# Two heads to a score pass in the forgetting attention, gate and up weights of an expert in one matmul and neighbouring rows in one packet, and the modulation's sums in three bf16 parts

## The chip, the cores and the metric

The kernel runs on one core of one Trainium2 chip. The metric is the device time of one execution in microseconds (us). The core has a matrix engine (PE, with its weight loads shown apart as PEld), a vector engine (DVE), a scalar engine (ACT), GpSimd (POOL), and queues that issue transfers (SP mostly, POOL for gathers and scatters). Transfers are carried out by 16 DMA engines, and the profile counts their packets.

## What is computed

512 tokens of width 1024 go through two layers of a first block and one layer of a second block, all in fp32. The parts that the change touches are these:

```python
mod = (silu(c) @ w_ada[i] + b_ada[i]).reshape(b, 6, d)      # modulation, two layers

def forgetting_mixer(h, ...):                               # layer 1: 16 heads of 64, causal
    logits = q @ k.T + (c_i[..., None] - cum[:, :, None, :])
    p = softmax(where(mask, logits, -1e30));  o = p @ v

def hierarchical_moe(h, ...):                               # both layers: 16 experts, width 256
    g_idx = argmax(softmax(t @ wg_r + bg_r)); top-2 of the 4 experts of that group
    hid = silu(t @ w_gate[e]) * (t @ w_up[e])               # 1024 -> 256, twice
    y += gate * (hid @ w_down[e])                           # 256 -> 1024
```

## The kernel before

The program runs in stages, and their times in the profiled execution are: layer 0's dilated attention (about 60 to 665 us), its output projection and router (to 722), its experts (to about 920), layer 1's forgetting attention (925 to 1245), output projection and router (to 1297), experts (to 1500), and the second block (to 1847).

**Products in three terms.** Almost every fp32 product is made of three matmuls on split operands (`split3`, L150, the matmul itself is L153): high x high, high x low, low x high. The split is an ACT copy into a reduced fp32 form (L315) and a DVE subtraction (L316).

**PE's order** is written by hand: in the attention stages a planner, `weave`, runs generators in lanes on a virtual clock. Each generator yields a cost and a delay from the table `DL` (in thousands), and while no lane is ready the planner emits background work, the next projections. The other engines' orders come from a scheduler.

**Modulation.** `ada_steps` (L232) reads 8 blocks of 128x512 of `w_ada`, and DVE accumulates them into `adacc` (L246, L248). Then four matmuls with a column of ones (L261) add up the 128 partitions, and DVE adds the bias (L264). 20 of the 24 blocks run as a lane in the dilated attention.

**Forgetting attention.** `mix_b` handles the heads in 8 pairs. A pair's projection, rows of q and k, and scores are lanes. `attn_forget` (L1367) handles one head: for each of 4 blocks of 128 queries it multiplies over the head's 64 dimensions (64 partitions) against 128 to 512 keys, three matmuls, then adds the causal mask with a bf16 matmul of an identity with a mask (`identb`, `maskb`, L1385, 128 partitions). DVE adds the bias and takes the sums (`pexp`, L473), ACT the exponential (L474); then `attn_values` transposes and multiplies with v. Score tiles `sc` are one of 3 buffers in PSUM. In the dilated attention both heads of a pair already take turns, one on the upper and one on the lower 64 partitions (L548).

**Experts.** `expert_loads` (L976) issues six transfers of 512 KB for each expert on SP's queue: gate and up in two halves each (k blocks of 128 rows, so that a packet is one row of 256 numbers, 1 KB), down in two (rows of 1024 numbers, 4 KB). `expert_split` makes high and low parts, except for expert 0. For an expert, `token_list` builds the list of at most 96 tokens from a one-hot matrix (L949), `token_gates` its gates (L957), POOL gathers the rows (L961). `step` runs `expert_half` (L1014) for gate and for up, each 8 k blocks x 3 matmuls of 256 columns; between the halves stand the next expert's transposes. Then come SiLU (L1026), the product, and the down projection (`expert_out`), whose rows POOL scatters and adds into `xd` (L966). Gathers read from `hd`, to which the router wrote the normed rows `hn` (L1194).

**The overflow branch.** `overflow` reads a flag on every engine and branches (L1070, L1071); its body is not entered here. It stands behind expert 0's transposes (L1008) and copies (`xTf`, L1010).

## Time and profile before

| | |
|---|---|
| Time, median of 3 runs | 1851.56 us (1849.99 to 1854.08) |
| Profiled execution | 1848.67 us, its span 1846.8 us |
| Mean granted clock of PE | 0.954 |
| PE busy | 1665.7 us (90%) |
| DVE busy | 1282.6 us (69%) |
| ACT busy | 926.5 us (50%) |
| POOL busy | 121.0 us (7%) |

The profile's span is 1.9 us shorter than the execution's own time. Busy shares are averages over the stages, and a stage has its own limit.

### The profile page before, as it was taken

The page shows a single profiled execution, that of the slowest core. Times are in us where ns is not written, and L with a number is a line of the kernel's source. Part 1 is how long each engine was busy: PE and PEld are TensorE (multiplying, and loading weights), DVE is VectorE, ACT ScalarE, POOL GpSimd, SP SyncE. Part 2 cuts the span into 40 slices and gives each one's busy share as a digit, 9 for nine tenths or more (in the row PEclk, how much of TensorE's full clock was granted, in tenths as well). Part 3 has the DMA queues.
Part 4 walks back from the last instruction along what each step waited for, and adds up shares of the span by engine and source line. Part 5 has one row for each costly group of instructions (what it writes and reads, how often), then busy time and mean ns, then how long its engine had stood idle before and what let it go on. Part 6 is the DMA issues. An engine that isn't in the chain of part 4 may idle for free. (4 is left out here: it accounts for less than half of the span.)

```text
span 1846.8 us, 30370 instructions
## 1 busy us (share of the span) xinstructions
PE 1665.7 (90%) x11022; PEld 1469.2 (80%) x11023; DVE 1282.6 (69%) x3181; ACT 926.5 (50%) x1978; POOL 121.0 (7%) x95
## 2 busy tenths in 40 slices
PE   5979999999999996999869999999598959999998
PEld 3878998989989985787658798888487748788886
DVE  6748777767686657787656667666687755998574
ACT  4536556555565643566444555552465533454443
POOL 1000000000000001133200000000133210000000
PEclk9989999999999997999988899899799979999999
DMA  8886655556564136899753221126699953333331
GB/s 291 244 276 183 189 159 176 164 154 195 153 184 132 58 113 211 270 316 302 208 148 93 58 69 58 63 70 212 197 315 313 295 154 110 98 105 88 112 118 76
DMA packets 294141, 310.83 MB, mean 168 GB/s; under 512 B 31263, under 2 KB 240779, under 8 KB 293980
## 3 DMA queue, kind: packets, MB, share of 16 engines
q1 hardware_dynamic: 286428, 291.88, 51.0%
q0 software_dynamic: 7552, 16.89, 4.2%
q8 instruction: 90, 1.47, 0.3%
q14 instruction: 71, 0.58, 0.1%
HBM read 287.62 MB, written 38.90 MB: 177 GB/s over the span
## 5 line engine op out<-in xcount | busy, mean ns | idle before, releaser
L153 PE MATMUL mm<-whi,hThi 128*128 128x384 f32 (+2 forms) x1128 | 403.3, 358 | 5.4 <-ACT hThi L739 2.0
L153 PE MATMUL mm<-whi,hTlo 128*128 128x384 f32 (+2 forms) x1128 | 384.3, 341 | 1.0 <-DVE hTlo L740 0.5
L153 PE MATMUL mm<-wlo,hThi 128*128 128x384 f32 (+2 forms) x1128 | 382.6, 339 | 0.0
L316 DVE TENSOR_TENSOR wlo<-wst,whi 128x768 fp32r<-128x768 f32 (+2 forms) x200 | 200.1, 1011 | 67.5 <-ACT whi L315 65.0
L153 PEld LDWEIGHTS mm<-whi,hThi 128*128 128x128 f32 x1128 | 215.6, 191 | 13.9 <-ACT hThi L739 3.2
L315 ACT ACTIVATE whi<-wst 128x768 fp32r<-128x768 f32 (+2 forms) x200 | 176.6, 892 | 87.6 <-PE mm L153 54.2
L153 PEld LDWEIGHTS mm<-whi,hTlo 128*128 128x128 f32 x1128 | 214.9, 191 | 6.2 <-DVE hTlo L740 3.3
L316 DVE TENSOR_TENSOR ehl<-est,ehl 128x1024 fp32r<-128x1024 f32 x144 | 175.8, 1222 | 60.8 <-ACT ehl L315 60.1
L153 PEld LDWEIGHTS mm<-wlo,hThi 128*128 128x128 f32 x1128 | 216.0, 191 | 1.9 <-issue 0.6
L315 ACT ACTIVATE ehl<-est 128x1024 fp32r<-128x1024 f32 x144 | 152.1, 1058 | 105.0 <-PE sc L153 23.3
L153 PE MATMUL mm<-ehl,xTh 128*96 128x256 f32 x960 | 178.4, 287 | 0.0
L248 DVE SCALAR_TENSOR_TENSOR adacc<-ast,csil,adacc 128x512 f32<-128x512 f32 x168 | 126.1, 751 | 64.9 <-DMA ast<-in_w_ada_dram 62.9
L153 PE MATMUL mm<-ehl,xTl 128*96 128x256 f32 x480 | 136.0, 283 | 0.0
L153 PEld LDWEIGHTS mm<-ehl,xTh 128*96 128x96 f32 x960 | 134.7, 165 | 0.0
L153 PE MATMUL mm<-hThi,whi 128*128 128x512 f32 (+1 forms) x288 | 107.2, 372 | 0.7 <-ACT sza L1887 0.6
L153 PE MATMUL mm<-hTlo,whi 128*128 128x512 f32 (+1 forms) x288 | 106.0, 368 | 0.5 <-DVE hTlo L310 0.3
L153 PE MATMUL mm<-hThi,wlo 128*128 128x512 f32 (+1 forms) x288 | 105.8, 367 | 0.0
L415 ACT ACTIVATE raw<-mm 128x256 f32<-128x256 f32 x126 | 48.2, 382 | 110.2 <-PE mm L153 109.8
L420 DVE TENSOR_REDUCE qss<-sq 128x4 f32<-128x256 f32 x128 | 53.0, 414 | 63.3 <-ACT sq L417 63.1
L153 PEld LDWEIGHTS mm<-ehl,xTl 128*96 128x96 f32 x480 | 79.0, 165 | 0.0
L1226 POOL MEMSET xg<- 96x1024 f32 x6 | 5.5, 952 | 1066.5 <-PE sc L153 1066.5
L966 POOL DMA_INDIRECT xd<-y,tidx x32 | 66.6, 2083 | 112.8 <-DVE hTl L1048 87.4
(488 smaller groups left out, 3568.0 us busy)
## 6 DMA issues: line engine op xcount, KB each, us to landing
ast<-in_w_ada_dram SPq DMA_DIRECT2D x192, 256.0 KB
wst<-in_a_w_in_dram SPq DMA_DIRECT2D x192, 192.0 KB
est<-in_w_gate_dram SPq DMA_DIRECT2D x64, 512.0 KB
est<-in_w_up_dram SPq DMA_DIRECT2D x60, 512.0 KB
wst<-in_w_in_dram SPq DMA_DIRECT2D x32, 512.0 KB
est<-in_w_down_dram SPq DMA_DIRECT2D x30, 512.0 KB
esp<-in_w_down_dram SPq DMA_DIRECT2D x30, 512.0 KB
wst<-in_b_w_in_dram SPq DMA_DIRECT2D x64, 192.0 KB
```

Source lines behind the costliest of these rows:

```text
L153: self.nc.tensor.matmul(out, lhsT=l, rhs=r, start=n_first and i == 0, stop=n_last and i == nt - 1)
L248: last = nc.vector.scalar_tensor_tensor(acc, st, self.csil[:, k:k + 1], acc, op0=ALU.mult, op1=ALU.add)
L315: nc.scalar.activation(hi, st, AF.Copy)
L316: nc.vector.tensor_sub(lo, st, hi.bitcast(F32))
L415: nc.scalar.activation(raw[:, t].rearrange("p a b -> p (a b)"), p[:, :256], AF.Copy)
L420: nc.vector.tensor_reduce(ss[:, 4 * t:4 * t + 4], sq.rearrange("p (g d) -> p g d", d=HD), axis=AX.X, op=ALU.add)
L966: self.nc.gpsimd.indirect_dma_start(out=dst, out_offset=bass.IndirectOffsetOnAxis(ap=idx, axis=0), in_=src, in_offset=None, bounds_check=S ...
L1226: nc.gpsimd.memset(xg, 0.0)
```

## The change

Seven edits go together.

1. **Scores of two heads.** `forget_scores` replaces the first half of `attn_forget`: both heads of a pair alternate matmul by matmul on the two halves of the partitions, in the groups of query blocks (0,1), (2), (3). The mask is added by 64-partition matmuls (`idh`, `maskh`), which POOL's queue loads by four transfers in `mix_b`. `forget_values` is a lane of its own; `DL` has new delays `bs` and `bp`; `pexp` has two buffers.
2. **Gate and up joined.** `expert_part` does gate and up in one matmul of 512 columns; it runs for k blocks 0 to 3, then the next expert's transposes, then 4 to 7.
3. **Neighbouring rows.** Partition p holds rows 8p to 8p+7. A tile holds two rows of gate and two of up, by two transfers of 256 KB whose packets are 2 KB. To match, L1194's result goes permuted into a second tile.
4. **Token list and gates in one product** for experts 2 to 15.
5. **Overflow's branch earlier,** ahead of the first expert's transposes and loads.
6. **The modulation's sums.** For the 20 blocks in the dilated attention POOL makes three bf16 parts of `adacc` (three copies, two subtractions, each on the result of the one before), and 12 bf16 matmuls add them up. `adacc` has one buffer.
7. **Small tiles** of `merge` have one buffer in place of two. The diff leaves out these, moved indices, and what it removes of `attn_forget` and `expert_loads`, which stand above.

```diff
@@ -42,6 +42,7 @@
+DL.update({'bs': 1.5, 'bp': 3.0})
@@ -248,9 +249,16 @@
                 self.ada_ins.append(last)
+        terms = [(acc, self.ones[:, 0:1])]
+        if later is True:
+            parts = self.t(pool, [P, 3, 512], BF16, "adp", 1)
+            for i in range(3):
+                nc.gpsimd.tensor_copy(parts[:, i], acc)
+                if i < 2:
+                    nc.gpsimd.tensor_sub(acc, acc, parts[:, i])
+            terms = [(parts[:, i], self.onesb[:, 0:1]) for i in range(3)]
         if later:
             yield 0, DL["ad"]
-        terms = [(acc, self.ones[:, 0:1])]
         if n_pe:
@@ -856,8 +864,9 @@
-                              ("tg", [P, NT, 16, 3], BF16)):
+                              ("tg", [P, NT, 16, 5], BF16)):
...
+        self.nc.gpsimd.tensor_copy(R["tg"][:, :, :, 0:2], self.tokv.unsqueeze(2).to_broadcast([P, NT, 16, 2]))
@@ -946,8 +955,11 @@
         for t in range(NT):
-            nc.tensor.matmul(p[:q, 0:2], lhsT=oh[:, t], rhs=self.tokv[:, t], start=t == 0, stop=t == NT - 1)
+            r = self.tokv[:, t] if tg is None else tg[:, t]
+            nc.tensor.matmul(p[:q, 0:r.shape[-1]], lhsT=oh[:, t], rhs=r, start=t == 0, stop=t == NT - 1)
         nc.vector.tensor_scalar(idx, p[:q, 0:1], p[:q, 1:2], 4096.0, op0=ALU.add, op1=ALU.add)
+        if tg is not None:
+            nc.vector.tensor_reduce(gate, p[:q, 2:5], axis=AX.X, op=ALU.add)
         return oh
@@ -976,28 +988,34 @@
+            for c in range(6):
+                plain = c == 5
+                shp = [P, 2, 2, F] if c < 4 else [P, 1, D]
+                j = i - DL["n0"]
+                if 0 <= j < DL["nx"]:
+                    st = self.t(self.px, shp, F32, f"x{j}")
+                else:
+                    st = self.t(self.ws, shp, F32, "esp" if plain else "est", DL["npl"] if plain else DL["nes"])
+                i += 1
+                if c < 4:
+                    for q, nm in enumerate(("w_gate", "w_up")):
+                        nc.sync.dma_start(st[:, q].rearrange("p k f -> p (k f)"),
+                                          dram_ap(a[nm], (l * 16 + e) * D * F + c * 2 * F, [[KC * F, P], [1, 2 * F]]))
+                else:
+                    nc.sync.dma_start(st, dram_ap(a["w_down"], (l * 16 + e) * D * F + (c - 4) * P * D, [[D, P], [P * D, 1], [1, D]]))
+                self.staged.append((self.W[e], st))
+                yield
...
+            pick = (lambda x: [x[:, :, k] for k in range(2)]) if len(w) < 4 else (lambda x: [x[:, 0]])
...
+                w.append([(x,) for x in pick(st)])
...
+            w.append(list(zip(pick(hl[:, 0]), pick(hl[:, 1]))))
@@ -1011,14 +1029,16 @@
-    def expert_half(self, p, o, x, w):
-        for k in range(KC):
+    def expert_part(self, p, x, w, ks):
+        w = [y for c in w[:4] for y in c]
+        for k in ks:
...
-            self.split3(p[:self.CAP, o:o + 256], terms, k == 0, k == KC - 1)
+            self.split3(p[:self.CAP].rearrange("p (a b) -> p a b", a=2), terms, k == 0, k == KC - 1)
@@ -1191,8 +1211,10 @@
                 self.route_tile(pn, lg[:, t], R, t)
-                nc.vector.scalar_tensor_tensor(h, h, r, shrow, op0=ALU.mult, op1=ALU.add)
-                nc.sync.dma_start(hd[ts, :], h)
+                ho = self.t(pn, [P, D], F32, "hn", 3)
+                by = lambda x: x.rearrange("p (q k) -> p k q", k=KC)
+                nc.vector.scalar_tensor_tensor(ho.rearrange("p (k q) -> p k q", k=KC), by(h), r, by(shrow), op0=ALU.mult, op1=ALU.add)
+                nc.sync.dma_start(hd[ts, :], ho)
                 if t == 0:
@@ -1228,15 +1250,15 @@
-            def listed(e):
+            def listed(e, both=False):
...
-                    ohs = self.token_list(pm, R["rk"][:, :, e], idx[:, e:e + 1], self.CAP)
+                    g = dict(tg=R["tg"][:, :, e], gate=gates[:, e:e + 1]) if both else {}
+                    ohs = self.token_list(pm, R["rk"][:, :, e], idx[:, e:e + 1], self.CAP, **g)
...
-                if e < 16:
-                    self.token_gates(ohs, [R["tg"][:, t, e] for t in range(NT)], gates[:, e:e + 1], self.CAP)
+                self.token_gates(ohs, [R["tg"][:, t, e, 2:5] for t in range(NT)], gates[:, e:e + 1], self.CAP)
@@ -1244,12 +1266,11 @@
                     p = self.mm()
-                    self.expert_half(p, 0, xs[e], w[0] + w[1])
+                    self.expert_part(p, xs[e], w, range(4))
                     if e < 15:
                         xs[e + 1] = self.expert_in(pm, xgs[(e + 1) % 3])
-                    self.expert_half(p, 256, xs.pop(e), w[2] + w[3])
-                    ohs = listed(e + 3)
-                    gated(e + 3, ohs)
+                    self.expert_part(p, xs.pop(e), w, range(4, KC))
+                    listed(e + 3, True)
                     hid = self.expert_hidden(pm, p)
@@ -1260,17 +1281,16 @@
+            ohs.append(listed(1))
...
-            load(2)
-            ohs.append(listed(1))
-            load(2)
+            self.overflow(pm, R, hd, l)
+            load(4)
...
-            self.overflow(pm, R, hd, l)
...
-            ohs.append(listed(2))
+            listed(2, True)
...
-            for e in range(3):
+            for e in range(2):
@@ -1364,37 +1384,57 @@
+    def forget_scores(self, pool, u, hp, before, then):
+        nc = self.nc
+        while not (u.get("rows") and self.have_cum and (before is None or before["done"])):
...
+        bias = [self.t(pool, [P, S], F32, f"biasF{h}", 1) for h in range(2)]
+        for h in range(2):
+            nc.sync.dma_start(bias[h], dram_ap(self.ncum, (2 * hp + h) * S, [[0, P], [1, S]]))
...
+        hs = [slice(h * HD, (h + 1) * HD) for h in range(2)]
+        z = [self.t(pool, [P, NT], F32, f"fzz{h}", 2) for h in range(2)]
+        d = [self.t(pool, [P, NT], F32, f"fdd{h}", 2) for h in range(2)]
+        blocks = [[], []]
+        for bs in ((0, 1), (2,), (3,)):
+            p = [self.sc(), self.sc()]
+            o, cost = 0, 300
+            for b in bs:
+                n = (b + 1) * P
+                q = slice(b * P, n)
+                for i, (x, y) in enumerate(((qh, kh), (qh, kl), (ql, kh))):
+                    for h in range(2):
+                        nc.tensor.matmul(p[h][:, o:o + n], lhsT=x[hs[h], q], rhs=y[hs[h], :n], start=i == 0, stop=False)
+                for c in range(2):
+                    for h in range(2):
+                        nc.tensor.matmul(p[h][:, o + b * P:o + n], lhsT=self.idh[hs[h], c], rhs=self.maskh[hs[h], c],
+                                         start=False, stop=c == 1)
+                o += n
+                cost += 200 + 1.4 * n
+            for h in range(2):
+                o = 0
+                for b in bs:
+                    n = (b + 1) * P
+                    e = self.t(pool, [P, n], F32, f"pexp{h}{b}", 2)
+                    self.softmax_piece(p[h][:, o:o + n], bias[h][:, :n], e, z[h][:, b:b + 1], d[h][:, b:b + 1], n)
+                    nc.vector.reciprocal(d[h][:, b:b + 1], d[h][:, b:b + 1])
+                    nc.vector.tensor_scalar(e, e, d[h][:, b:b + 1], None, op0=ALU.mult)
+                    blocks[h] += [e[:, k * P:(k + 1) * P] for k in range(b + 1)]
+                    o += n
+            if bs[-1] == NT - 1:
+                u["scored"] = 2
+            yield cost, DL["bs"]
+        then(blocks)
+    def forget_values(self, pool, u, hp, oT, blocks):
+        nc = self.nc
...
+        hs = [slice(h * HD, (h + 1) * HD) for h in range(2)]
+        terms = [[(vh, vl, kb, b * (b + 1) // 2 + kb) for kb in range(b + 1)] for b in range(NT)]
+        yield from self.attn_values(pool, "b", blocks, hs, terms, lambda h, o: nc.scalar.activation(oT[hs[h], hp], o, AF.Copy))
+        u["done"] = 2
@@ -1413,6 +1453,11 @@
+            self.idh, self.maskh = [self.t(pq, [P, 2, P], BF16, nm) for nm in ("idh", "maskh")]
+            for out, off in ((self.idh, OFF_ID), (self.maskh, OFF_MASK)):
+                for h in range(2):
+                    nc.gpsimd.dma_start(out[h * HD:(h + 1) * HD],
+                                        dram_ap(self.a["c_tab"], off, [[N_CONST, HD], [HD * N_CONST, 2], [1, P]]))
@@ -1449,8 +1494,8 @@
-                    for h in range(2):
-                        fg.append((h, self.attn_forget(pa, u, hp, h, oT), DL["bu"] + h * DL["bo"]))
+                    fg.append(("scores", self.forget_scores(pa, u, hp, hist[hp - 2] if hp > 1 else None, lambda blocks: fg.append(
+                        ("values", self.forget_values(pa, u, hp, oT, blocks), DL["bp"]))), DL["bu"]))
@@ -2158,7 +2199,7 @@
-                self.dilated(po, pa, hT, oT, first, begun, [lambda l=l, cb=cb: self.ada_steps(pa, l, cb, later=True) for l, cb in todo])
+                self.dilated(po, pa, hT, oT, first, begun, [lambda l=l, cb=cb: self.ada_steps(pa, l, cb, n_st=2, n_acc=1, later=True) for l, cb in todo])
...
```

The order of three places follows, before and then after the change.

PE in the forgetting attention, the first head's first two query blocks before (`sc` is the score tile, `kTh`/`kTl` the keys' high and low parts):

```order
L153 MATMUL sc_12291<-kTh_2537_12260,qTh_2534_12245 128x128
L153 MATMUL sc_12291<-kTl_2538_12261,qTh_2534_12245 128x128
L153 MATMUL sc_12291<-kTh_2537_12260,qTl_2535_12246 128x128
L1385 LDWEIGHTS identb_432
L1385 MATMUL sc_12291<-maskb_434,identb_432 128x128
L153 MATMUL sc_12301<-kTh_2537_12260,qTh_2534_12245 128x256
L153 MATMUL sc_12301<-kTl_2538_12261,qTh_2534_12245 128x256
L153 MATMUL sc_12301<-kTh_2537_12260,qTl_2535_12246 128x256
L1385 LDWEIGHTS identb_432
L1385 MATMUL sc_12301<-maskb_434,identb_432 128x128
```

PE at the same place after (two score tiles, one for each head):

```order
L1409 MATMUL sc_12208<-kTh_2547_12173,qTh_2544_12158 128x128
L1409 MATMUL sc_12209<-kTh_2547_12173,qTh_2544_12158 128x128
L1409 MATMUL sc_12208<-kTl_2548_12174,qTh_2544_12158 128x128
L1409 MATMUL sc_12209<-kTl_2548_12174,qTh_2544_12158 128x128
L1409 MATMUL sc_12208<-kTh_2547_12173,qTl_2545_12159 128x128
L1409 MATMUL sc_12209<-kTh_2547_12173,qTl_2545_12159 128x128
L1412 LDWEIGHTS idh_11518
L1412 MATMUL sc_12208<-maskh_11519,idh_11518 128x128
L1412 LDWEIGHTS idh_11518
L1412 MATMUL sc_12209<-maskh_11519,idh_11518 128x128
L1412 LDWEIGHTS idh_11518
L1412 MATMUL sc_12208<-maskh_11519,idh_11518 128x128
```

The two heads alternate, and the mask of a block is four matmuls in place of one. The groups that follow, (2) and (3), stand behind 12 projection matmuls each at this place.

PE in the dilated attention, where the modulation's sum stands before, in the middle of a projection:

```order
L153 MATMUL mm_5116<-whi_4684,hTlo_325 128x384
L261 MATMUL tp_5133<-ones_65,adacc_5009 128x1 x4
L153 MATMUL mm_5116<-whi_4684,hThi_324 128x384
```

PE at such a place after (the start of the 12 bf16 matmuls), and then POOL ahead of it:

```order
L154 MATMUL av_1536<-pTl_1483,vhi_219_862 64x128
L154 MATMUL av_1536<-pTh_1482,vlo_220_863 64x128
L269 LDWEIGHTS adp_1430
L269 MATMUL tp_1562<-onesb_430,adp_1430 128x1
L269 LDWEIGHTS adp_1430
L269 MATMUL tp_1562<-onesb_430,adp_1430 128x1
L269 LDWEIGHTS adp_1430
L269 MATMUL tp_1562<-onesb_430,adp_1430 128x1
```

```order
L256 CAST adp_1430<-adacc_1407 128x512
L258 TENSOR_TENSOR adacc_1407<-adacc_1407,adp_1430 128x512
L256 CAST adp_1430<-adacc_1407 128x512
L258 TENSOR_TENSOR adacc_1407<-adacc_1407,adp_1430 128x512
L256 CAST adp_1430<-adacc_1407 128x512
```

The sum is 12 weight loads and matmuls where there were 4, and they read what POOL's fifth instruction leaves.

ACT at the start of layer 0's experts before, from the last early splits of weights to the branch (`x` and `est` are weight tiles, `tp` the transposes of expert 0's rows):

```order
L315 ACTIVATE ehl_9560<-x_1781_8750 128x1024
L315 ACTIVATE ehl_9565<-x_1809_8885 128x1024
L1010 ACTIVATE xTf_8985<-tp_8986 128x384
L1010 ACTIVATE xTf_8985<-tp_8992 128x384
L1070 TENSOR_LOAD rt_anyi_8937
L1071 COMPARE_AND_BRANCH
```

ACT there after, with the branch's body left out:

```order
L323 ACTIVATE ehl_9838<-x_1802_9037 128x1024
L323 ACTIVATE ehl_9844<-x_1831_9174 128x1024
L323 ACTIVATE ehl_9851<-est_9712 128x1024
L1090 TENSOR_LOAD rt_anyi_9226
L1091 COMPARE_AND_BRANCH
...
L1028 ACT_TABLE_LOAD
L1028 ACTIVATE xTf_9726<-tp_9727 128x384
L323 ACTIVATE ehl_9857<-est_9715 128x1024
L1028 ACTIVATE xTf_9726<-tp_9733 128x384
L323 ACTIVATE ehl_9863<-est_9718 128x1024
```

The copies of expert 0's rows moved behind the branch and behind one more split, of a tile that SP issues just ahead of its own branch, and a table load now stands ahead of them.

## Rows read from the trace of the kernel before

**Rows 1.** Windows: the two attentions, then both experts' stages; columns in us, then clock, DMA share, GB/s.

```profile
140.00:660.00 520.00, 503.12 (x3762) 479.37 (x3760) 370.74 (x950) 295.86 (x756) 0.00 (x0) 1.00 0.52 155
945.00:1245.00 300.00, 290.89 (x1901) 252.38 (x1900) 194.26 (x632) 153.25 (x383) 0.00 (x0) 0.94 0.24 68
770.00:920.00 150.00, 139.78 (x1003) 114.55 (x1001) 114.98 (x171) 85.07 (x132) 44.14 (x25) 0.99 0.93 281
1340.00:1480.00 140.00, 130.36 (x959) 109.18 (x959) 113.02 (x164) 84.77 (x127) 42.65 (x24) 0.98 0.99 304
```

**Rows 2.** Chain that ended last: start us, us, what; layer 1's experts, second block.

```profile
1352.08 2.83 PE mm L153 x24
1355.05 0.18 PE tp L957 x4
...
1370.78 13.54 DMA est<-in_w_down_dram
...
1817.26 10.88 PE mm L153 x48
```

**Rows 3.** SiLU of the 16 experts, layer 0, then layer 1.

```profile
L1026 ACT ACTIVATE sg<-mm x16: 361/380/383, 751.0 to 915.0; 96x256 f32<-96x256 f32 x16
...
L1026 ACT ACTIVATE sg<-mm x16: 364/381/383, 1325.5 to 1488.7; 96x256 f32<-96x256 f32 x16
```

**Rows 4.** Main DMA queue in 1560:1580, 1340:1380 and 1260:1300: packets, MB, share.

```profile
q1 hardware_dynamic: 3312, 2.23, 39.2%
...
q1 hardware_dynamic: 8052, 10.49, 80.2%
...
q1 hardware_dynamic: 3712, 7.87, 56.0%
```

**Rows 5.** PE's longest wait at the start of layer 0's experts.

```profile
PE tp L949 <- PEq L1071: 5.6, 1, 5.6
```

**Rows 6.** Timeline of ACT, then of PE, at the start of layer 0's experts.

```profile
733.99 1.06 ACT L315 ACTIVATE ehl<-est 128x1024 fp32r<-128x1024 f32 x1 [1.09 <-DMA est<-in_w_gate_dram]
749.75 1.28 ACT L1026 ACT_TABLE_LOAD   x1
...
736.97 1.15 PE L153 MATMUL mm<-est,xTf 128*96 128x256 f32 x2
```

**Rows 7.** L1194 by source: count, min/median/max ns, first and last start.

```profile
L1194 DVE SCALAR_TENSOR_TENSOR hn<-hn,tn_r,rh x8: 1274/1277/1283, 691.8 to 1291.7; 128x1024 f32<-128x1024 f32 x8
```

**Rows 8.** Timeline in the dilated attention: bf16 sums of `merge`, last `adacc`, its sum.

```profile
164.14 0.56 PE L640 MATMUL tp<-s,perm 128*128 128x12 bf16 x16
...
199.75 0.75 DVE L248 SCALAR_TENSOR_TENSOR adacc<-ast,csil,adacc 128x512 f32<-128x512 f32 x1
...
205.66 0.95 PE L261 MATMUL tp<-ones,adacc 128*128 128x1 f32 x8
```

**Rows 9.** POOL by line, an instruction of 128x512.

```profile
L1638 POOL MEMSET tt<- 128x512 f32 x1 | 0.5, 528 | 0.0
```

**Rows 10.** Timeline of PE: one head's scores, then a dilated pair's.

```profile
1046.62 0.32 PE L153 MATMUL sc<-kTh,qTh 64*128 64x128 f32 x1
...
1049.77 0.64 PE L153 MATMUL mm<-whi,hThi 128*128 128x384 f32 x1
...
605.92 0.39 PE L548 MATMUL sc<-kTh,qTh 64*128 64x256 f32 x2
606.14 0.28 PE L548 MATMUL sc<-kTl,qTh 64*128 64x256 f32 x2
...
606.62 0.28 PE L548 MATMUL sc<-kTh,qTl 64*128 64x256 f32 x2
606.83 0.27 PE L153 MATMUL av<-pTh,vhi 128*64 128x128 f32 x1
```

**Rows 11.** A window in the forgetting attention, columns as in rows 1.

```profile
1050.00:1060.00 10.00, 10.00 (x31) 7.69 (x32) 5.68 (x23) 3.70 (x12) 0.00 (x0) 0.50 0.17 53
```

**Rows 12.** DVE by line in the forgetting attention: score tiles read.

```profile
L473 DVE CUSTOM_DVE_ANT_0 pexp<-sc,biasF 128x128 f32<-128x128 f32 (+1 forms) x64 | 31.2, 490 | 23.4 <-PE sc L1385 22.7 <-DMA biasF<-ncum 0.7
```

66 lines of the change are left out of this document (11 added, 55 removed).

## The prediction

> **What bounds the kernel now.** I read the page first: PE is busy nine tenths of the span, DVE seven tenths, POOL hardly at all (the table above). Then the windows by stage, because the stages have different limits [rows 1]. In the dilated attention PE works 503 of 520 us at full clock: whatever comes off PE there comes off the time. In the forgetting attention it works 291 of 300, but the clock granted is 0.94 on average, so some 18 us of those 300 are lost to the clock. In the experts PE works 140 of 150 and 130 of 140 us, and there the DMA engines are busy 0.93 and 0.99 of the time. The chain shows which of the two ends last: runs of matmuls, and between them transfers of weights that PE waits for, one piece of 13.54 us [rows 2]. 16 experts' SiLUs lie 164.0 and 163.2 us apart from first to last [rows 3], 10.9 us an expert, some of them paced by PE and some by a transfer.
>
> **The change part by part.**
>
> *Gate and up, packets.* The main queue's share over its packets gives a price. 0.392 x 16 engines x 20 us / 3312 is 37.9 ns for a packet of 673 bytes; 63.7 ns at 1303; 96.6 ns at 2120 [rows 4]. A line through the ends has 10.6 ns for a packet and 0.0406 ns for a byte, and meets the middle at 63.5. So 1 KB costs 52.2 ns and 2 KB 93.7. An expert's gate and up are 2048 packets before, 2048 x 52.2 / 16 = 6.68 us, and 1024 after, 6.00 us: 0.68 us less. About 13 experts of a layer are loaded while the engines are full: 8.9 us a layer, 18 in both. The extra transfers that SP issues (four an expert) are hidden, since SP waits for buffers.
>
> *Gate and up, matmuls.* 24 matmuls of 256 columns took 2.83 us, 118 ns each, and 48 of 512 columns 10.88 us, 227 ns each [rows 2]. 24 x 227 = 5.45 us stands for 48 x 118 = 5.66: 0.21 less, and the joined list and gates save four small matmuls, 0.18 [rows 2]. 0.39 us an expert is worth something only where no transfer is late, and most of it is waited away at the next late transfer. If packets are no cheaper, only the last three experts keep it: 2 x 3 x 0.39 = 2 us. If it adds in full at six experts of a layer, 18 + 5 = 23. I take -18, with -2 and -23 as ends.
>
> *The start of the experts.* PE waits 5.6 us for the branch, behind the wait for the gather [rows 5]; put ahead, the branch runs while the rows are gathered. But ACT now copies expert 0's rows only after the split of a tile that lands at 733.99 in layer 0 and takes 1.06 us, then its branch (taken as 1 us, between nothing and PE's 5.6), then a table load of 1.28 us, and the copy itself, 384 columns where the split's 1.06 us are 1024, so 0.4: 737.7 in all. The first expert matmul starts at 736.97 before [rows 6]. What is late next is ACT, not PE. I take +1 for both layers together; if the tile comes earlier, -4; if the branch takes ACT as long as PE, +6.
>
> *Permuted rows.* L1194 takes 1.28 us [rows 7] and runs eight times; only the last of a layer lies on the path. Reading with a step of 8 numbers may cost nothing or double it: 0 to 2.6 us, I take +1, which holds POOL's four new small transfers too: they stand near the last scatter, which could be a microsecond late.
>
> *The modulation's sums.* A sum takes PE 0.95 us, and 16 bf16 loads and matmuls with few columns 0.56 [rows 8]. 12 are 0.42, so 0.5 us less, and of 20 sums about 16 stand where PE is full: -8 (from -4, if small matmuls drain badly, to -10). POOL's chain is the open price. The trace has no copy or subtraction on POOL. The nearest rows: a POOL fill of the same tile takes 0.528 us [rows 9], so five are 2.6; DVE's accumulation of that tile takes 0.75 [rows 8], so five at twice that are 7.5. The time available is seen in the timeline: `adacc` is done at 200.50, its sum starts at 205.66 [rows 8]; 5.16 us is the shortest of 13 such gaps, the longest of them 5.8. The first two blocks have little, in a stretch where PE isn't full, so I count a third of the chain for each; the other five have far more. I take 4.5 us, between the ends and nearer the fill, since three of five instructions read one operand: the chain fits in all but the first two, 2 x 1.5 = +3. At 7.5 it is 13 x (7.5 - 5.4) + 2 x 2.5 = +32. If the first two are covered as well it is 0.
>
> *Scores of two heads.* One head's scores, from the first matmul to the projection behind, take 1049.77 - 1046.62 = 3.15 us at full clock; a pair 6.3. Two heads on two halves of the partitions take, in the dilated attention, 0.12 us for a step of 2 x 256 columns (from 606.14 to 606.62 four steps), and a run of six 0.91 [rows 10], so 0.19 for entering and leaving. A pair has 3 x 1280 columns a head: 15 steps of 256, 1.8 us; 8 mask steps of 128, 0.5; three entries, 0.6: 2.9 us. 3.4 us less for each of 8 pairs: -27, from -20 if the mask's weight loads aren't hidden and cost 0.05 us each, 16 a pair, to -30.
>
> A rule of the Trainium skill bears on this. In "TensorEngine Tiling (Array Packing)", Overview, a contraction of at most 64 run as two row tiles is at most twice as fast. The trace goes past it: one head's run has 3 x 1280 + 512 columns in 3.15 us, 2.2 us for 3072, where the paired run does 3072 in 0.91 [rows 10] (the single run has a mask after each block). By the bare factor of two this term would be 8 x 3.15 = 25 us.
>
> *The clock.* It is 0.50 from 1050 to 1060 [rows 11], right behind a head's scores, and 18 us of the stage are lost this way [rows 1]. In the dilated attention, with scores of two heads, the clock was 1.00 throughout [rows 1]. But 18 us lost at 0.50 are 36 us of low clock, three or four such stretches, so some of the eight pairs keep their clock with single heads too. I take back most of it, -13, with 0 and -17 as ends.
>
> *New waits there.* A group takes two of three score tiles, so the next group waits until DVE has read the first head's: on average 0.49 us a read [rows 12], against about 2 us of projection between groups, so it waits only when DVE is behind. Two or three runs of transposes now stand without projection ahead of the values. +5, from 0 to +15.
>
> The sum: -18 + 1 + 1 - 8 + 3 - 27 - 13 + 5 = -56. The profiled execution took 1848.67 us, so 1792.7; the median lies 2.9 higher, 1795.6. I predict 1796.
>
> **The rivals.**
>
> *Packets of 2 KB are no cheaper by the byte.* Then 16 us of the sum are missing: 1812. For it: the full stretch's engines already move 10.49 MB in 40 us [rows 4], and the gathers' queue takes its share. Against it: the line through three rows. This is what a page of the Trainium skill would have: "DMA: Bandwidth & Descriptors", Specifications, puts full rate at transfers of 512 bytes and more. The trace does not agree so far, since 2120-byte packets have 45.6 ns a KB and 1303-byte ones 48.9.
>
> *POOL's chain is longer than the gap.* At 7.5 us, 29 more than in my sum: 1825. For it: five instructions in a row with a wait each, on an engine of which no such row exists. Against it: the fill at 0.53. The Trainium skill speaks against the change here: "GPSIMD Engine Reference", Performance versus the Vector engine, has a two-operand instruction there 1.96 times as long as on the vector engine. No run here shows that yet; an estimate from it with 0.75 us is 1.47 for each of two subtractions.
>
> *The forgetting attention gives little.* The clock stays low after scores and the groups wait for DVE: 0 instead of -13, +15 instead of +5: 1819. For it: DVE and ACT wait on each other at every piece. Against it: DVE works 194 of 300 us.
>
> *Slower than before.* POOL's chain holds up PE so long that all is eaten: 13 (c - 5.4) + 2c/3 must reach 56 + 3 = 59, so c = 9.5 us; from 9.7 it is slower by over 0.2%. At 10.5 us it is 66 + 7 = 73, so 1866. That would be 2.1 us an instruction, four times the fill. Little speaks for it, unless DVE, 71% busy in this stage, and POOL hold each other up.
>
> *The merged list and gates, the small tiles* move nothing I can price; if they cost a wait, it is inside the range.
>
> **How the numbers follow.** Forecast 0.55 (1775 to 1812 as its own range), packets 0.15, POOL's chain 0.12, the forgetting attention 0.12, slower 0.06 (some of that between). The range, 1770 to 1830, takes in the first four with their ends and leaves out the slower case, the tails of two of the rivals, and the case that all gains reach their far ends. About 0.2%, 3.7 us, is what a measurement here can tell from no change. Faster by more 0.92, within it 0.03, slower 0.05.
>
> **What would show it.** Packets: SiLUs some 154 to 155 us apart instead of 164, DMA engines still full. Joined matmuls: 24 of 512 columns in about 5.45 us. Start: first expert matmul within 2 us of now, ACT the one waited for. Sums: POOL rows under 1 us on average, no wait of PE for `adp` outside the first two blocks; waits of 2 us at 13 places would show the second rival. Scores: a pair under 3 us, no window at 0.50 from 1000 to 1230; PE waits for DVE at score tiles would show the third. I am wrong if the dilated attention doesn't get shorter by about 6 us, the forgetting one by about 35, the experts by about 9 a layer.

## The result, and the profile after

| | before | changed |
|---|---|---|
| Time, median (6 runs each) | 1852.39 us (1848.83 to 1854.84) | 1861.03 us (1858.46 to 1864.74) |
| Ratio to before, 95% interval | | 1.0051, 1.0034 to 1.0068 |
| Span of the profiled execution | 1846.8 us | 1858.2 us |
| Mean granted clock of PE | 0.954 | 0.951 |

The prediction said 1796 us and 3% faster; the kernel became half a per cent slower. Where the 11.4 us between the spans of the two profiled executions come from is seen by following the same instructions through both traces. The router's first transposes behind the dilated attention start at 683.4 us before and at 730.0 after: +46.6. From there to the first SiLU +3.5; over layer 0's 16 experts -5.9; to layer 1's first SiLU -28.5 (the forgetting attention); over layer 1's experts -6.4; to the end +2.1. So the gains that were forecast exist, somewhat smaller, and one stage ate more than all of them.

Windows of the changed kernel, first the dilated attention, then the forgetting attention (it begins later now); columns as in [rows 1]:

```profile
140.00:660.00 520.00, 467.55 (x3533) 446.24 (x3534) 346.10 (x891) 270.85 (x696) 76.00 (x91) 0.95 0.51 151
995.00:1295.00 300.00, 280.33 (x2150) 253.57 (x2149) 206.64 (x682) 153.74 (x402) 0.38 (x1) 0.98 0.30 88
```

In the dilated attention PE was busy 503 of 520 us at clock 1.00 [rows 1] and is busy 468 at 0.95: it waits, and it runs more slowly. In the forgetting attention the clock rose from 0.94 to 0.98. The SiLUs, in the form of [rows 3], lie 158.1 and 156.8 us apart where they were 164.0 and 163.2:

```profile
L1046 ACT ACTIVATE sg<-mm x16: 361/380/385, 801.1 to 959.2; 96x256 f32<-96x256 f32 x16
...
L1046 ACT ACTIVATE sg<-mm x16: 359/380/387, 1341.2 to 1498.0; 96x256 f32<-96x256 f32 x16
```

What PE waits for in 140 to 700 us, first in the changed kernel, then in the kernel before (us in total, times, longest):

```profile
PE tp L494 <- DVE nat L652: 27.3, 6, 5.1
PE sc L613 <- DVE sR L481: 16.0, 7, 4.8
PE sc L556 <- DVE zN L481: 6.5, 6, 1.2
```

```profile
PE tp L486 <- DVE nat L644: 2.6, 5, 1.1
PE sc L605 <- DVE sR L473: 2.0, 2, 1.2
PE sc L548 <- DVE zN L473: 1.1, 3, 0.5
```

PE does not wait for POOL at all. It waits for DVE, at score tiles and at `merge`. What DVE itself waits for in the same stretch, changed kernel:

```profile
DVE adacc L249 <- DMA ast<-in_w_ada_dram: 62.7, 59, 2.4
DVE adacc L247 <- POOL adp L256: 47.0, 17, 4.1
```

The second line is new. L247 is the first multiplication of the *next* block. One such place in the timeline of the changed kernel (start, length, instruction, idle time before it and its releaser):

```profile
213.47 0.45 PE L269 MATMUL tp<-onesb,adp 128*128 128x1 bf16 x12
214.15 0.75 DVE L249 SCALAR_TENSOR_TENSOR adacc<-ast,csil,adacc 128x512 f32<-128x512 f32 x1 [1.21 <-DMA ast<-in_w_ada_dram]
215.06 0.62 POOL L256 CAST adp<-adacc 128x512 bf16<-128x512 f32 x1 [17.17 <-DVE adacc L249]
215.35 0.15 DVE L272 TENSOR_TENSOR mod<-tp,vcol 128x4 f32<-128x4 f32 x1
215.76 1.16 POOL L258 TENSOR_TENSOR adacc<-adacc,adp 128x512 f32<-128x512 f32 x1
...
218.90 0.61 POOL L256 CAST adp<-adacc 128x512 bf16<-128x512 f32 x1
219.54 0.49 DVE L247 TENSOR_SCALAR adacc<-ast,csil 128x512 f32<-128x512 f32 x1 [4.04 <-POOL adp L256]
223.04 1.13 PE L613 MATMUL sc<-kT,qT 64*128 64x128 f32 x14 [2.09 <-DVE sR L481]
```

POOL's chain takes 4.45 us from 215.06 to 219.51, as the prediction had assumed (4.5). DVE stands still for 4.04 us of it, since the instruction at the head of its queue overwrites `adacc`, which POOL still reads. Behind it in the queue stand readings of score tiles, and PE's scores at 223.04 wait for those.

### The profile page after: what moved, and what is told of

It reads as the page before. It is cut to its first block, busy times and chain, and to the rows that moved or that the text cites. A ratio compares the mean times of both kernels' runs of the same rounds, so it can differ in the third digit from the quotient of the medians.

```text
span 1858.2 us, 29413 instructions
## 1 busy us (share of the span) xinstructions
PE 1627.2 (88%) x10302; PEld 1384.9 (75%) x10303; DVE 1286.1 (69%) x3181; ACT 920.1 (50%) x1975; POOL 209.8 (11%) x201
## 5 line engine op out<-in xcount | busy, mean ns | idle before, releaser
L154 PE MATMUL mm<-whi,hThi 128*128 128x384 f32 (+2 forms) x1128 | 407.6, 361 | 3.2 <-ACT hThi L747 1.3
L154 PE MATMUL mm<-ehl,xTh 128*96 128x512 f32 x480 | 153.5, 401 | 0.0
L494 PE MATMUL tp<-cst,pexp 128*128 128x128 f32 x400 | 66.3, 286 | 45.8 <-DVE nat L652 27.3
L256 POOL CAST adp<-adacc 128x512 bf16<-128x512 f32 x60 | 37.4, 623 | 533.1 <-DVE adacc L249 199.0
L154 PE MATMUL mm<-ehl,xTl 128*96 128x512 f32 x240 | 94.8, 395 | 0.0
L154 PEld LDWEIGHTS mm<-ehl,xTh 128*96 128x96 f32 x480 | 73.4, 162 | 25.8
L494 PEld LDWEIGHTS tp<-cst,pexp 128*128 128x128 f32 x400 | 47.7, 144 | 56.6 <-DVE nat L652 29.2
```

Source lines behind the costliest of these rows:

```text
L154: self.nc.tensor.matmul(out, lhsT=l, rhs=r, start=n_first and i == 0, stop=n_last and i == nt - 1)
L256: nc.gpsimd.tensor_copy(parts[:, i], acc)
L494: nc.tensor.transpose(p[:, j * q:(j + 1) * q], blocks[c + j], self.ident[:q, :q])
```

## The experiments

Marker of the dilated attention: the start of the router's first transposes, 683.4 us before and 730.0 in the changed kernel. "All but the sums" below is e3.

**e1, e3: the sums in fp32 again**, with two buffers of `adacc` as before, and with one.

```diff
-        if later is True:
+        if False:
```

(e1 also has n_acc=2 for these blocks.) 

> The changed kernel with only the modulation's sums put back: four fp32 matmuls on adacc, two adacc buffers, nothing on POOL. Theory (buffer): in the changed kernel DVE's first multiplication of the next block waits for POOL to let go of the only adacc (47 us of DVE in the dilated attention), and all that is queued behind it on DVE is late for PE; without it the dilated attention ends as before (first transposes of the router at about 683 us, 730 now) and the other stages keep what they gained (about 25 in the forgetting attention, 17 in the experts): about 1810. Rival (elsewhere): the loss in the dilated attention comes from the single small tiles of merge or another edit, and at least 20 us of it stay: 1830 or more.

> As e1 (four fp32 matmuls, nothing on POOL) but with one adacc buffer. DVE's order then has the next block's first multiplication behind the sum of its own predecessor. Theory (buffer and place in the queue): one buffer costs only where the first multiplication stands ahead of what frees it; here it stands right behind the add that needs the same sum, so within 10 us of e1. Rival (one buffer is dear by itself): transfers of w_ada start later and DVE waits: 25 us or more above e1.

e1: 1828.45 us, ratio 0.9868 (0.9838 to 0.9899), marker 687.6. e3: **1816.98 us, ratio 0.9806 (0.9775 to 0.9836)**, marker 683.7. The sums in three parts thus cost the whole loss, some 44 us (1861.0 against 1817.0); one buffer of `adacc` without POOL costs nothing. In size both expectations missed: e1 came out 18 us above its 1810, just under the rival's 1830, and e3 is 11 us faster than e1, of which the markers hold 4; the rest was not traced. Windows of e3 in the dilated attention:

```profile
140.00:660.00 520.00, 500.67 (x3740) 476.66 (x3739) 372.14 (x946) 291.57 (x744) 1.05 (x1) 1.00 0.53 156
```

**e2: two buffers of `adacc`** in the changed kernel, room taken from `UN` (one buffer for two).

```diff
-... self.ada_steps(pa, l, cb, n_st=2, n_acc=1, later=True)
+... self.ada_steps(pa, l, cb, n_st=2, n_acc=2, later=True)
```

> The changed kernel with POOL's three parts kept, but two adacc buffers; room for the second comes from UN (result of the near attention), one buffer instead of two. Theory (buffer): DVE no longer waits for POOL at L247, the chain of 4.4 us fits into the gap ahead of the sums, and 12 bf16 matmuls save about 8 us against e1: about 1803, router's first transposes at about 675. Rival (chain): the 4.4 us of POOL hold up PE themselves or slow DVE down; then 1840 to 1861.

1857.78 us, ratio 1.0017 (0.9994 to 1.004), marker 715.0. DVE's wait shrank and did not go:

```profile
DVE adacc L247 <- POOL adp L256: 27.0, 12, 3.7
```

The time is in the rival's range (1840 to 1861): that a second `adacc` would cure it fell here.

**e4: POOL's work without a result.** e1, and POOL does three copies and two subtractions per block into a tile that nobody reads, so that no engine needs the result.

```diff
+            scratch = self.t(pool, [P, 512], BF16, "adp", 1)
+            for i in range(3):
+                nc.gpsimd.tensor_copy(scratch, acc)
+                if i < 2:
+                    nc.gpsimd.tensor_sub(scratch, acc, self.cst[:, 0:512])
```

> As e1 (fp32 sums, two adacc buffers), and POOL does five instructions of the same size for each of the 20 blocks, reading adacc and writing to a tile that nobody reads. Theory (buffer): POOL's work by itself costs nothing, within 4 us of e1. Rival (contention): POOL and DVE slow each other, 20 us or more above e1, DVE's rows in the dilated attention longer.

1864.66 us, ratio 1.006 (1.0038 to 1.0082), marker 725.9: the marker is 38 us behind e1's, and DVE has no wait for POOL. DVE's own instructions became longer. One place in e4's timeline:

```profile
254.90 1.30 POOL L258 TENSOR_TENSOR adp<-adacc,cst 128x512 bf16<-128x512 f32 x1
254.95 1.27 DVE L661 TENSOR_TENSOR me<-mz,nat 128x8 f32<-128x8 f32 x1
```

An instruction on 8 numbers a partition takes 1.27 us; it starts just after POOL's subtraction and ends with it. Before, this form took 0.159 us on average (8 of them in 140 to 700 us).

**e12: only copies on POOL,** e1 with seven copies a block, unused.

```diff
+            for i in range(7):
+                nc.gpsimd.tensor_copy(scratch, acc)
```

> As e4 (fp32 sums, two adacc buffers, POOL's results unused), with seven copies for a block in place of three copies and two subtractions: the same time on POOL, only one operand each. Theory (turns with any POOL instruction): DVE's instructions with two operands in SBUF wait for copies too, 20 us or more above e1. Rival (only POOL's two-operand instructions collide): within 6 us of e1.

1840.87 us, ratio 0.9928 (0.9897 to 0.9959), marker 703.6: 12 us behind e1, 16 at the marker, between what the two theories expected (20 or more, and at most 6). Copies hold DVE up too, though less than copies with subtractions (DVE's `raw<-raw,qr` took 1368 ns on average here, 1530 in e4, 1224 before).

**e5: the same parts made by DVE.**

```diff
-                nc.gpsimd.tensor_copy(parts[:, i], acc)
+                nc.vector.tensor_copy(parts[:, i], acc)
-                    nc.gpsimd.tensor_sub(acc, acc, parts[:, i])
+                    nc.vector.tensor_sub(acc, acc, parts[:, i])
```

> The changed kernel with the three bf16 parts made by DVE in place of POOL (three copies, two subtractions), one adacc buffer, 12 bf16 matmuls. Theory (POOL and DVE in each other's way: POOL's instructions and DVE's with two operands in SBUF take turns, and DVE's first multiplication stands in its queue waiting for POOL): DVE gets about 50 us more work in a stage where it is busy 71%, but no turns and no wait between engines; the dilated attention ends within 10 us of e3 (first transposes of the router at 684): 1808 to 1827. Rival (any lateness of the sum costs): a chain ahead of the sums holds up PE wherever it runs: 1840 or more.

1881.85 us, ratio 1.0131 (1.0083 to 1.0178), marker 743.3. DVE by line and PE's two longest waits of e5 in 140 to 700 us:

```profile
L258 DVE TENSOR_TENSOR adacc<-adacc,adp 128x512 f32<-128x512 f32 x36 | 24.8, 688 | 0.8
L256 DVE CAST adp<-adacc 128x512 bf16<-128x512 f32 x54 | 22.9, 423 | 1.0
```

```profile
PE tp L676 <- ACT eb L671: 26.1, 6, 5.8
PE tp L494 <- DVE nat L652: 18.0, 6, 3.1
```

47.7 us of work more on DVE moved the marker by 59.6 us against e3. DVE, 71% busy on average in this stage [rows 1], had no room for it. The theory, which had the kernel within 10 us of e3 once POOL was out of the way, fell. The rival had the time, but not the place: PE has no wait at the sums (L269) here.

**e8: one part only.** The changed kernel with one copy and four bf16 matmuls a block (the second and third part of the sums are left out).

```diff
-            for i in range(3):
+            for i in range(1):
```

> The changed kernel with only the first of the three bf16 parts: one copy on POOL for each block, four bf16 matmuls; it leaves out the second and third part of the sums. Theory (time on POOL): DVE waits 0.7 us at a block where it waited 2.8 us, PE is held up little, and the time falls most of the way to e3: 1812 to 1828. Rival (the wait for another engine as such, or the order): 1845 or more.

1818.9 us, ratio 0.9813 (0.9772 to 0.9854), marker 678.9; DVE waits 5.2 us in all for POOL. A chain of 0.61 us is free. Against e3 the marker gained 4.8 us, with four short matmuls a sum.

**e10, e13: more buffers.** e10 gives the parts two buffers (room from `UN`, and from `bias`, three for four); e13 gives both `adacc` and the parts two (room also from `pexp`, three for four). **e14** is e3 with e13's room taken, the base for e13.

```diff
-            parts = self.t(pool, [P, 3, 512], BF16, "adp", 1)
+            parts = self.t(pool, [P, 3, 512], BF16, "adp", 2)
```

> The changed kernel (POOL's three parts, one adacc) with two buffers for the parts; room comes from one buffer less of UN and of the bias tiles. Theory (place in the queues): in the changed kernel POOL starts a block's parts only when the sum of the block before has freed the parts' only buffer, which is just when DVE comes to its next first multiplication; with two buffers POOL starts when adacc is done, DVE's wait for POOL falls from 47 us to under 10, but POOL then works while DVE does, and the two take turns as in e4, which alone cost 40 us: 1835 to 1860. Rival (the buffer alone): without the wait the kernel is faster than e3, 1805 to 1815.

> The changed kernel with two buffers each for adacc and for the three parts; the room comes from UN (1 buffer), pexp (3) and bias (3). Both theories expect DVE's first multiplication of a block to wait for POOL no more (under 10 us in the stage, 47 with single buffers), since a chain of 4.4 us then has a whole block, over 20 us. Theory A, the waits of DVE behind the chain were the whole price: the router's first transposes come at 680 to 695 and the kernel takes 1815 to 1830. Theory B, POOL's work also holds up DVE where the two run at once, as in the run with POOL's work unused (router's transposes at 726, small two-operand DVE instructions of 1.1 us on average): short instructions of merge again over 0.5 us on average, the router's transposes at 710 to 730, the kernel at 1845 to 1870.

> The kernel with fp32 sums and one adacc (1817 us), with the same room taken from UN (1 buffer), pexp (3) and bias (3), nothing else. It is the base that the run with both buffers doubled is to be read against. If the room costs nothing, 1815 to 1823. If score tiles or merge wait for a buffer, 1828 to 1845, and that much of the run with two buffers for the parts (1879 us, UN 1 and bias 3) was the room and not POOL.

e10: 1878.99 us, ratio 1.0133 (1.0077 to 1.019), marker 743.5. e13: 1862.77 us, ratio 1.0056 (1.0039 to 1.0073), marker 729.3. e14: 1825.29 us, ratio 0.9859 (0.982 to 0.9899), marker 685.3, so the room costs 2 us there (its median lies 8 above e3's, with a wide spread). e10 missed both its theory and its rival: DVE's wait, expected under 10 us, grew. It is shown in e10, then in e13:

```profile
DVE adacc L247 <- POOL adp L256: 54.8, 18, 4.6
```

```profile
DVE adacc L247 <- POOL adp L256: 25.8, 13, 3.7
```

Both theories had expected this wait gone in e13, and both were wrong. The timeline of e13 shows why:

```profile
228.25 0.75 POOL L256 CAST adp<-adacc 128x512 bf16<-128x512 f32 x1 [24.45 <-PE tp L269]
228.97 0.15 DVE L272 TENSOR_TENSOR mod<-tp,vcol 128x4 f32<-128x4 f32 x1
...
232.22 0.61 POOL L256 CAST adp<-adacc 128x512 bf16<-128x512 f32 x1
232.86 0.48 DVE L247 TENSOR_SCALAR adacc<-ast,csil 128x512 f32<-128x512 f32 x1 [3.74 <-POOL adp L256]
```

The blocks' accumulations run ahead of PE's sums until every buffer is in use. Then POOL's chain starts only when PE's sum of an earlier block frees a buffer, and DVE's next block stands at the head of its queue until the chain ends, with one buffer or with two. Counted through the traces, a sum of the kernel before leaves one finished block unsummed behind it; a sum of e2 or e10 mostly one or two, of e13 two or three; in the changed kernel it is none or one.

**e15: one tile for `adacc` and its parts,** one buffer. The tile is free only when PE has summed, so the next block's multiplication stands behind the sum (as in e3), and the chain lies ahead of the sum.

```diff
-                acc = self.t(pool, [P, 512], F32, "adacc", n_acc)
+                both = self.t(pool, [P, 1280 if later is True else 512], F32, "adacc", n_acc)
+                acc = both[:, 0:512]
-            parts = self.t(pool, [P, 3, 512], BF16, "adp", 1)
+            parts = both[:, 512:1280].bitcast(BF16).rearrange("p (a b) -> p a b", a=3)
```

> The changed kernel with adacc and its three parts in one tile, one buffer, so that DVE's first multiplication of a block stands behind the sum of the block before, as in the run with fp32 sums and one adacc (1817 us), and POOL's chain of 4.4 us lies between the last accumulation and the sum, a gap of about 5.6 us there. Both theories expect DVE's wait for POOL ahead of a block's first multiplication to vanish (47 us in the changed kernel). Theory A, that wait was the whole price of the sums: router's first transposes at 680 to 690, the kernel at 1812 to 1822. Theory B, POOL's work beside DVE's costs as much as where its result was unused: short DVE instructions of merge or of the norms several times as long, router's transposes at 705 to 730, the kernel at 1840 to 1865. In between (690 to 705), PE waits for the chain at the sum, which the waits would show.

1846.55 us, ratio 0.9964 (0.9948 to 0.998), marker 714.2. DVE's wait for POOL is gone, and PE waits 0.3 us once for it. Still the marker is 30.5 us behind e3, as theory B had it. DVE and POOL by line of e15, 140 to 700 us, then the first of these rows in the kernel before:

```profile
L444 DVE TENSOR_TENSOR raw<-raw,qr 128x1024 f32<-128x1024 f32 x21 | 33.2, 1579 | 0.4
L170 DVE SCALAR_TENSOR_TENSOR qn_t<-qn_t,qv 128x16 f32<-128x16 f32 x21 | 7.4, 354 | 0.0
L670 DVE TENSOR_TENSOR me<-me,mz 128x16 f32<-128x16 f32 x8 | 6.2, 774 | 0.3
...
L257 POOL CAST adacc<-adacc 128x512 bf16<-128x512 f32 x57 | 50.6, 887 | 411.2 <-DVE qn_t L170 174.5 <-DVE s L640 123.3 <-DVE nat L653 110.9
L259 POOL TENSOR_TENSOR adacc<-adacc 128x512 f32<-128x512 f32 x38 | 49.3, 1297 | 3.1
```

```profile
L435 DVE TENSOR_TENSOR raw<-raw,qr 128x1024 f32<-128x1024 f32 x21 | 25.7, 1224 | 0.5
```

Both engines are slower where they run at once. In the changed kernel POOL's copies take 613 ns on average and its subtractions 1163, and DVE's `raw<-raw,qr` 1221: there DVE stands still meanwhile, so nothing is drawn out.

One more place in e15 shows which of the two is drawn out:

```profile
166.71 1.16 POOL L259 TENSOR_TENSOR adacc<-adacc 128x512 f32<-128x512 f32 x1
166.93 0.97 DVE L670 TENSOR_TENSOR me<-me,mz 128x16 f32<-128x16 f32 x1
167.82 0.94 DVE L325 TENSOR_TENSOR wlo<-wst,whi 128x768 fp32r<-128x768 f32 x1
167.93 1.30 POOL L257 CAST adacc<-adacc 128x512 bf16<-128x512 f32 x1
```

`me<-me,mz` starts behind POOL's subtraction and ends with it. `wlo<-wst,whi`, two operands in SBUF as well, starts 0.11 us ahead of POOL's copy and keeps its 0.94 us; the copy takes 1.30 instead of 0.61. Between 140 and 690 us `wlo<-wst,whi` lies beside a copy that started after it at 13 places, and each time it is the copy that is longer, 1.30 to 1.37 us. At these places the one that starts second pays.

**e6: 1 KB packets.** e3 with each transfer of gate and up cut into two of 128 KB, one row to a packet.

```diff
-                        nc.sync.dma_start(st[:, q].rearrange("p k f -> p (k f)"), ... + c * 2 * F, [[KC * F, P], [1, 2 * F]]))
+                        for k in range(2):
+                            nc.sync.dma_start(st[:, q, k], ... + (c * 2 + k) * F, [[KC * F, P], [1, F]]))
```

> As e3 (fp32 sums with one adacc buffer, everything else changed), with gate and up in twice as many transfers whose packets are 1 KB as before the change; matmuls joined as in the change. Theory (packets): each expert's transfers take 0.7 us more, the 16 SiLUs of a layer lie 6 to 9 us further apart than in e3, 12 to 18 us in all: about 1831. Rival (joined matmuls): the experts' gain comes from PE's side, packets don't matter: within 4 us of e3, 1817.

1845.79 us, ratio 0.9948 (0.9924 to 0.9971). Layer 0's SiLUs in e6, then in e3:

```profile
L1046 ACT ACTIVATE sg<-mm x16: 360/377/386, 754.1 to 928.2; 96x256 f32<-96x256 f32 x16
```

```profile
L1046 ACT ACTIVATE sg<-mm x16: 359/380/382, 753.7 to 914.3; 96x256 f32<-96x256 f32 x16
```

174.1 against 160.6 us, and in layer 1 175.4 against 159.2: 13.5 and 16.2 us more. That is not the price of the packets alone. The kernel before had packets of 1 KB too, in a quarter of e6's transfers for gate and up, and its SiLUs lay 164.0 and 163.2 us apart. The main queue tells the same, in 770:910 of the kernel before, 820:955 of the changed kernel and 770:910 of e6:

```profile
q1 hardware_dynamic: 26415, 34.65, 76.0%
...
q1 hardware_dynamic: 15841, 34.70, 75.1%
...
q1 hardware_dynamic: 26706, 32.33, 74.7%
```

Share x 16 engines x window over MB is 49.1 us of one engine for a MB before, 46.7 with packets of 2 KB, and 51.8 in e6. The packets give 2.4 of the 5.1 us by which e6 stands above the changed kernel; the other 2.7 came with e6's smaller transfers or their order in memory, which this run doesn't separate.

**e7: scores of one head,** e3 with `attn_forget` and its lanes as before.

```diff
-    fg.append(("scores", self.forget_scores(pa, u, hp, ...), DL["bu"]))
+    for h in range(2):
+        fg.append((h, self.attn_forget(pa, u, hp, h, oT), DL["bu"] + h * DL["bo"]))
```

> As e3, with the forgetting attention as before the change (one head's scores at a time, mask on 128 partitions). Theory: the forgetting attention's part of the change is worth the 25 us by which that stage got shorter in the changed kernel, so about 1842, with windows of the clock at 0.50 again. Rival (shifted work): the stage's length hangs on DVE and the planner's order, and one head costs less than 12 us: below 1829.

1844.54 us, ratio 0.9961 (0.9938 to 0.9984): the scores of two heads, their clock and their new waits are together worth 27.6 us. The clock is back at 0.95 in 940:1240, where e3 has 0.98 in 947:1247.

**e9, e11: small buffers.** e3 with two buffers of `merge`'s small tiles again, and e3 with five buffers for the forgetting values' transposed probabilities.

```diff
-            hi = self.t(pool, [P, min(n, 4) * q], F32R, tag + "h", {"hT": 2, "xT": 4}.get(tag, 3))
+            hi = self.t(pool, [P, min(n, 4) * q], F32R, tag + "h", {"hT": 2, "xT": 4, "pB": 5}.get(tag, 3))
```

> As e3, with merge's small tiles in two buffers as before the change. Theory (queue on DVE, not these tiles): within 4 us of e3, 1817. Rival (small tiles): merge's chain waits for its own old tiles, and the dilated attention gets 10 us or more shorter.

> As e3, with five buffers in place of three for the transposed weights of the forgetting attention's values. Theory (new waits there): PE's 11.7 us of waiting for DVE at transposes (seven times) come from the second head's copies, which wait for the first head's products to free the buffers; about 10 us less, and the low-clock windows behind these waits go as well: 1802 to 1810. Rival (DVE is behind anyway): within 4 us of e3.

1818.56 us (0.9793, 0.974 to 0.9845) and 1816.46 us (0.9786, 0.9731 to 0.9841): no difference from e3. e11 missed: the wait that it was to remove stayed as long as in e3, so the number of these buffers doesn't cause it. That DVE's subtraction itself comes late is the rival's reading, and was not followed further:

```profile
PE tp L494 <- DVE pBl L496: 11.7, 7, 5.4
```

## Why the prediction was wrong

**The step that failed** is POOL's term of the modulation's sums: "the chain fits in all but the first two, 2 x 1.5 = +3", with -8 for PE. The net -5 was measured as +46.6 at the marker (in e3, without the edit, +0.3). PE's own part came: the sums keep PE busy for 8.5 us between 140 and 700 us, where it was 18.4. So did the signs that the prediction named for this term: POOL's rows are 0.83 us on average, and PE has no wait for `adp`. None of them watched DVE. Three things in the term were wrong.

*The gap was between two different blocks.* The prediction read `adacc` done at 200.50 and its sum at 205.66 as one block [rows 8]. The order of DVE's instructions in the program before (the first of each block and the end of each sum, others left out) has them apart; `tp_296` is PE's sum of `adacc_270`:

```
L246 TENSOR_SCALAR adacc_270_1133<-ast_269_1131,csil_5_80 128x512
L246 TENSOR_SCALAR adacc_326_1397<-ast_325_1395,csil_5_80 128x512
L264 TENSOR_TENSOR mod_6_82<-tp_296_1257,vcol0_9_88 128x4
L246 TENSOR_SCALAR adacc_403_1794<-ast_402_1792,csil_5_80 128x512
```

`adacc_326` is begun, and in the trace finished, before the sum of `adacc_270` is taken. With two buffers the accumulation was a block ahead of its sum, so PE never was the one to wait for POOL. The one who waits is DVE, which wants the buffer for the next block, and the place that DVE's queue gives to that first multiplication is right behind the sum that frees a buffer.

*The buffers were priced at nothing.* "`adacc` has one buffer" stood in the change, and the prediction asked only who reads the chain's result, not who needs its input's buffer. With one `adacc` DVE's next block waits for the whole chain. The chain itself starts when its block is accumulated and PE's sum of the block before has freed the parts; the sum is the later of the two at 6 of 20 blocks in the changed kernel and at 19 in e2. By e2, e10 and e13 more buffers alone don't help: the accumulations run further ahead, and DVE comes to its first multiplication before the chain has ended.

*The mean of DVE's load was taken for slack.* The rule that spoke against the change was named and weighed only as a longer duration. The nearest case in the prediction, "unless DVE, 71% busy in this stage, and POOL hold each other up", was given no price of its own, though it is what e4, e12 and e15 show. The duration of the chain was right, 4.45 us against 4.5. The threshold of 9.7 us that was worked out for a slower kernel didn't hold, since it assumed that PE waits and that a chain costs nothing as long as it fits a gap.

One account fits these runs: what DVE loses between 140 and 700 us, as waits for POOL, as its own instructions drawn out beside POOL's (each form's mean against e3, times its count, up to 690 us), or as work of its own, and what the marker loses against e3's 683.7.

| run | DVE waits for POOL | drawn out | own work | marker later |
|---|---|---|---|---|
| changed kernel | 47.0 | 0 | | 46.3 |
| e2, two `adacc` | 27.0 | 4.6 | | 31.3 |
| e4, work unused | 0 | 26.4 | | 42.2 |
| e5, on DVE | | | 47.7 | 59.6 |
| e8, one part | 5.2 | | | -4.8 |
| e10, two of parts | 54.8 | | | 59.8 |
| e12, copies | 0.8 | 13.4 | | 19.9 |
| e13, both two | 25.8 | 5.3 | | 45.6 |
| e15, one tile | 0 | 27.6 | | 30.5 |

Between 1.0 and 1.6 us are lost for each us of DVE's, but for e8. Against nearer bases, e1 for e4 and e12 and e14 for e13, the last column is 38.3, 16.0 and 44.0. It is a sum that fits, and no run varies DVE's loss alone. A part of the excess is the clock: the granted clock in 140 to 660 us is 0.94 to 0.97 in the runs that lose 30 us or more and 1.00 in e3. How much of it is the clock and how much the place of the loss was not separated.

The Trainium skill states the cause of what is drawn out: "GPSIMD Engine Reference", Specifications, has POOL's way to SBUF shared with the vector engine and in contention with DVE's instructions that have two SBUF inputs. The runs agree: the eight forms that e15 drew out by more than 1 us in all have two operands in SBUF, and those that read PSUM kept their means (`pTl<-tp,pTh` within 0.1 us in sum over 44 instructions). `wlo<-wst,whi` has two such operands and kept its mean too: there POOL's copy was the one drawn out, as the place at 167.82 shows. The prediction's estimate from "Performance versus the Vector engine" of that page of the Trainium skill, 1.47 us for a subtraction, was too long: 1.16 measured.

**The other terms.**

*Packets and joined matmuls, -18:* the SiLUs came 5.9 and 6.4 us closer in the changed kernel (3.4 and 4.0 in e3), -12 instead of -18. That larger packets are cheaper by the byte was right, and the rival that they are not fell: 46.7 us of one engine for a MB instead of 49.1. The size was wrong. An expert's three matrices are 3.15 MB, so 2.4 x 3.15 / 16 = 0.47 us an expert, not 0.68, and 6.1 for the prediction's 13 experts of a layer. That is close to what the SiLUs of the changed kernel show, with nothing left over for the joined matmuls.

*Start of the experts, +1, and permuted rows, +1:* +3.5 from the marker to layer 0's first SiLU. The first expert matmul starts 60.0 us behind the marker, 53.6 before, so the sign "within 2 us of now" failed. ACT is waited for, as forecast ("PE tp L959 <- ACT xTf L1028", 3.8 us), but a longer wait, which the prediction did not have, stands ahead of it: "PE tp L1026 <- DVEq L1091", 7.6 us, which the profile puts down to the branch on DVE and into which the gather falls too, where PE waited 4.8 for the gather and 5.6 for its own branch before. L1216 came out near the upper end, 2.26 us at the median where L1194 took 1.28 [rows 7]:

```profile
L1216 DVE SCALAR_TENSOR_TENSOR hn<-hn,tn_r,rh x8: 2046/2255/2352, 738.2 to 1310.1; 128x1024 f32<-128x1024 f32 x8
```

*Scores of two heads, -27:* right in size. A pair's three groups in the changed kernel, each from its first matmul to what follows it:

```profile
1042.45 0.33 PE L1409 MATMUL sc<-kTh,qTh 64*128 64x128 f32 x2
...
1043.60 0.44 PE L154 MATMUL mm<-whi,hThi 128*128 128x384 f32 x1
...
1045.90 0.44 PE L1409 MATMUL sc<-kTh,qTh 64*128 64x384 f32 x2
...
1046.75 0.44 PE L154 MATMUL mm<-whi,hThi 128*128 128x384 f32 x1
...
1049.04 0.50 PE L1409 MATMUL sc<-kTh,qTh 64*128 64x512 f32 x2
...
1050.06 0.66 PE L455 MATMUL tp<-cst,raw 128*128 128x128 f32 x4
```

They take 1.15, 0.85 and 1.02 us, 3.0 together, read as the prediction read the single head; 2.9 was forecast.

*Clock, -13, and new waits, +5:* clock 0.98 where it was 0.94 gives back about 12 of 300 us. The waits were larger than +5: PE waits 11.7 us in seven pieces at the values' transposes for DVE's subtraction and 2.5 in two more, where such waits took 2 us before. Together -28.5 where -35 was forecast; e7 has the three terms as -27.6.

Without the sums, 51 us were forecast. e3 is 36 us faster by its ratio (0.0194 x 1852), and its profiled span is 31.8 us shorter: +0.3 to the marker, +2.4, -3.4, -28.5, -4.0 and +1.4 in the stretches named above.

## What to carry to other kernels

When a step goes to an idle engine, ask who needs the *input's* buffer back, what stands behind that instruction in its queue, and whether the step's start hangs on the consumer of the block before; "the result is ready in time" answers only half. A gap read between "done" and "used" must be checked for belonging to the same buffer. An engine's mean load over a stage says nothing on whether work can be added: here 2.4 to 2.7 us a block on DVE, with a busy share of 71%, cost their length or more.

## What the runs showed of the hardware that was not expected

DVE's instructions with two operands in SBUF and POOL's drew each other out where both ran at once, and at the places followed it was the later one that waited for the earlier: 128x8 on DVE from 0.16 to 1.27 us beside a subtraction on POOL (e4), POOL's copy of 128x512 from 613 to 887 ns on average, its subtraction from 1163 to 1297, DVE's 128x1024 multiplication `raw<-raw,qr` from 1224 to 1579 (e15). Copies alone on POOL did it to about half the extent (13.4 us against 26.4). Reading with a step of 8 numbers made a DVE instruction of 128x1024 take 2.26 us instead of 1.28.
